# The order of ScalarE's and VectorE's work on a bank of transposed rows

## The chip, the cores and the metric

The kernel runs on one core of one Trainium2 chip. The metric is the device time of one execution in microseconds (us). A core has five engines with an instruction queue each, worked off in order: TensorE (PE in the profile; its weight loads are PEld), VectorE (DVE), ScalarE (ACT), GpSimd (POOL) and SyncE (SP). Matmul results land in PSUM, which has eight banks; a bank holds 512 f32 numbers in each of 128 partitions.

## The reference, cut to what matters

One layer of a decoder is computed for a prompt of 1024 rows and for eight sample rows with a paged cache of 8192 positions each. The change touches the prompt alone, at the two places where normed rows go into the next projection:

```
xp = xp + merge_heads(fox_prompt(...), sgu_prompt(...), g_att_out, g_sgu_out, w_o)
xp = xp + cross_attend(rmsnorm(xp, g_cross), mk, mv, w_cq, w_co)
f, conv_p = conv_ffn(rmsnorm(xp, g_ffn), zeros, w_up, conv_w, conv_b, w_down)
xp = xp + f
```

The model width is 1024 and all numbers are f32.

## The kernel before, in words

**Products.** Each large product is made of three matmuls in a reduced format: every f32 operand is split into a rounded part h and a remainder l, and h·h + h·l + l·h is summed (`gemm3`, lines 272 to 274). The helper `split` makes the two parts. ScalarE rounds (line 235, or line 238 where each row is multiplied by a gain on the way), and VectorE subtracts the rounded part from the source (line 236, or 239 with the gain). Weights come through SyncE's queue into buffers `wr` (line 249) and are split into `wh` and `wl` on lines 235 and 236.

**Tiling of the prompt.** The 1024 rows are worked on in two halves of 512 rows. For each half there is an output projection (`out_proj`, lines 1063 to 1065 and 1081 to 1083), then cross attention (`cross`), a second output projection inside it, and the MLP (`ffn`). A half has four blocks of 128 rows.

**The seam.** `norm_T` turns the finished rows so that the next product can use them. It is called four times in the kernel: into cross attention and into the MLP, for each half of the prompt. One call goes through two pairs of row blocks (`t0` = 0 and 2), and in each pair through four banks (`kk` = 0, 2, 4, 6). Into one bank TensorE puts four transposes of 128x128 (line 1124): columns 0 to 255 belong to feature block kk, columns 256 to 511 to feature block kk+1. `split` is then called once for each half of the bank (line 1129), with the gain of that feature block. So one call of `norm_T` has 8 banks and 16 splits, and the kernel has 64.

In the text below A0 and A1 are ScalarE's roundings of the first and second half of a bank (line 238, 128x256), and V0 and V1 are VectorE's remainders of these halves (line 239, 128x256).

**What comes behind a seam.** After the four banks of a pair, `first` runs the first product of the next stage on these 256 columns (`gemm3_late`): first all matmuls that need only rounded rows (lines 280 and 281), then those that need the remainders (line 284). The products after it go through `gemm3`.

**What comes ahead of it.** The second output-projection column goes block by block; the sum with the residual is line 1015, its squares are line 230, and `factor` (line 1031 on ScalarE, line 1032 on GpSimd) gives the scale of a row block, which `scaled` (line 1037) or, for the last two blocks, `both` (line 1044 on ScalarE, line 1045 on VectorE) applies. The last pair of transposes waits for `both`; eight matmuls without use (`fill`, line 1102) stand ahead of them.

**What sets the order.** The program is written as generators that yield an estimated duration; a loop at the end mixes in the steps of the sample rows (the decode), whose VectorE work on gathered cache pages is on lines 1444 and 1448, whose matmuls into `dv` are on line 1495, and whose gathers GpSimd issues on lines 1428 and 1489. The framework then orders the instructions of every engine by a simulated timeline when the kernel is built, with priorities (`tc.high_priority` stands around the transposes and the splits of a bank), and adds the waits between engines. On the chip this order is fixed.

Of the kernel before, what the change touches and what calls it, by code (L numbers as in the profile page):

```python
# [7 lines left out]
F32 = mybir.dt.float32  # L8
# [3 lines left out]
AF = mybir.ActivationFunctionType  # L12
ALU = mybir.AluOpType
# [65 lines left out]
def build(nc, tc, ctx, a, phases=None):  # L79
# [31 lines left out]
    def U(shape, dt=F32):  # L111
        n = 1
        for s in shape[1:]:
            n *= s
        t = upool.tile([P, UW], dt, tag="u", bufs=NU, name=nm("u"))[:, :n]
        if len(shape) == 3:
            t = t.rearrange("p (a b) -> p a b", b=shape[2])
        return t
# [50 lines left out]
    gp = const.tile([P, G_W], F32, tag="gp", name="gp")  # L169
# [62 lines left out]
    def split(src, h, l, scale=None):  # L232

        if scale is None:
            nc.scalar.activation(h, src, AF.Copy)  # L235
            nc.vector.tensor_tensor(l, src, h.bitcast(F32), op=ALU.subtract)  # L236
        else:
            nc.scalar.activation(h, src, AF.Copy, scale=scale)
            nc.vector.scalar_tensor_tensor(l, src, scale, h.bitcast(F32), op0=ALU.mult, op1=ALU.subtract)  # L239
# [858 lines left out]
    def fill(tr, hs):  # L1098

        for k in range(8):  # L1100
            with tc.issue_after(newest(ENG.PE)):
                mmul(tr[:, :256], hs[k][:, 0:P], hs[k][:, 0:256], start=True, stop=True)

    def norm_T(ys, g0, first):


        hs, ls = [], []
        for t0 in (0, 2):
            c = slice(t0 * P, (t0 + 2) * P)
            late = callable(ys[t0])  # L1110
            if late:
                ys[t0:] = ys[t0]()
            for kk in range(0, 8, 2):
                if t0 == 0:
                    h2, l2 = U([P, 2, 512], F32R), U([P, 2, 512], F32R)
                    hs += [h2[:, 0, :], h2[:, 1, :]]
                    ls += [l2[:, 0, :], l2[:, 1, :]]
                tr = TR()
                if late and kk == 0:
                    fill(tr, hs)  # L1120
                with tc.high_priority():
                    for q in range(2):
                        for i in range(2):
                            nc.tensor.transpose(
                                tr[:, (q * 2 + i) * P : (q * 2 + i + 1) * P], ys[t0 + i][:, (kk + q) * P : (kk + q + 1) * P], ident
                            )
                    for q in range(2):
                        k = kk + q
                        split(tr[:, q * 256 : (q + 1) * 256], hs[k][:, c], ls[k][:, c], scale=gp[:, g0 + k : g0 + k + 1])
                yield 0.6  # L1130
            first(hs, ls, c)
            if t0 == 0:
                yield 3
        held[0] = False
        return hs, ls


    def cross(xt, sq):
# [19 lines left out]
        def first(hs, ls, c):  # L1158
            gemm3_late([(ps[:, c], pairs(ws, d, hs, ls, c)) for d, ps in enumerate(begun)])

        hs, ls = yield from norm_T(xt, G_CROSS, first)
        r = rows_rstd(sq, 0, 4)
        rq = sm([P, 4], "rq", 2)
# [105 lines left out]
    def ffn(hf, xt, ys, late=None):  # L1269
# [6 lines left out]
        def first(hs, ls, c):  # L1276
            gemm3_late([(pv[:, c], pairs(w, hs, ls, c)) for w, pv in begun.values()])

        hs, ls = yield from norm_T(ys, G_FFN, first)
        if hf:  # L1280

# [753 lines left out]
```

## Time and profile before

| | |
|---|---|
| time, median of 3 runs | 1794.42 us (1788.66 to 1794.93) |
| time of the profiled execution | 1793.69 us |
| its span in the profile | 1791.7 us, so 2.0 us lie around it |
| TensorE clock over the span | 0.993 of full speed |
| VectorE, ScalarE, GpSimd busy | 78%, 41%, 27% of the span |
| cross attention, first and second half | seams at about 521 to 548 us and 1154 to 1187 us |
| MLP, first and second half | seams at about 684 to 708 us and 1321 to 1343 us |

A row of the timeline gives the start in us, the duration, the engine, the line of the kernel, the operation, output and inputs with their shapes, the number of instructions merged in the row, and in brackets how long the engine stood idle ahead of it and what ended that. Instructions on ScalarE and VectorE overlap a little at their ends, so the next one of the same kind starts 0.1 us before the one ahead of it has ended.

### The profile page before, as it was taken

How to read it: one execution, taken by the hardware profiler on the slowest of the kernel's cores; microseconds unless marked ns; L12 is line 12 of the kernel's file. 1: busy time of each engine (PE TensorE's matmuls, PEld its weight loads, DVE VectorE, ACT ScalarE, POOL GpSimd, SP SyncE). 2: the span in 40 equal slices, each digit the busy share in tenths (PEclk: the TensorE clock that was granted, in tenths of full speed). 3: DMA queues.
4: the chain of work that ended last, by engine and by line, in shares of the span. 5: the costliest groups of instructions: out<-in, count | busy, mean ns of one | idle time of the engine just before them, and what ended most of it. 6: DMA issues, size and time to landing. Idle time of an engine off the chain costs nothing.

```text
span 1791.7 us, 25124 instructions
## 1 busy us (share of the span) xinstructions
PE 1735.9 (97%) x9653; PEld 1285.7 (72%) x9653; DVE 1399.9 (78%) x1733; ACT 733.5 (41%) x1374; POOL 488.3 (27%) x461
## 2 busy tenths in 40 slices
PE   8999999889999999999999999999999999999997
PEld 5787777655677666767777777766666778768875
DVE  4689658989788986989999999898885549855344
ACT  6332355566643635333333244335353233333232
POOL 1252234443222332333322223433322112102110
PEclk9999999999999999999999999999999999999999
DMA  8786798777697975779788788988879587568982
GB/s 291 297 304 226 294 334 319 259 264 244 254 403 279 363 299 224 282 285 345 290 301 313 291 317 311 376 306 346 320 280 350 214 306 249 191 260 297 359 310 80
DMA packets 157074, 521.06 MB, mean 291 GB/s; under 512 B 20874, under 2 KB 40842, under 8 KB 124186
## 3 DMA queue, kind: packets, MB, share of 16 engines
q0 software_dynamic: 57168, 341.14, 50.0%
q1 hardware_dynamic: 92874, 165.73, 26.5%
q10 hardware_dynamic: 6912, 12.59, 1.9%
q8 instruction: 76, 1.25, 0.3%
q14 instruction: 44, 0.36, 0.1%
HBM read 495.47 MB, written 23.93 MB: 290 GB/s over the span
## 4 chain that ended last, share of the span: by engine, by line
PE 53%; issue 9%; DMA 8%; DVE 6%; ACT 2%; POOL 2%; POOLq 0%; DVEq 0%; ACTq 0%; SPq 0%
DMA kv<-cache_v,io 6%; PE ba L272 6%; PE ba L274 6%; PE ba L273 6%; PE dv L1495 4%; PE bb L272 3%; PE bb L273 3%; PE bb L274 3%; PE ba L1063 1%; DVE s L1448 1%; PE ba L1064 1%; PE ba L1065 1%; PE dv L331 1%; DMA kv<-cache_k,io 1%; PE dv L1774 1%
## 5 line engine op out<-in xcount | busy, mean ns | idle before, releaser
L235 ACT ACTIVATE wh<-wr 128x1024 fp32r<-128x1024 f32 (+2 forms) x220 | 228.6, 1044 | 443.3 <-PE ba L273 142.3
L236 DVE TENSOR_TENSOR wl<-wr,wh 128x1024 fp32r<-128x1024 f32 (+2 forms) x220 | 262.7, 1200 | 165.1 <-PE ba L274 57.4
L1428 POOL DMA_INDIRECT kv<-cache_k,io x128 | 186.9, 1460 | 606.8 <-DVE s L1448 327.2
L1444 DVE TENSOR_TENSOR kv<-kv,d 128x1024 f32<-128x1024 f32 (+1 forms) x156 | 258.0, 1681 | 32.6 <-DMA kv<-cache_k,io 32.6
L1448 DVE TENSOR_REDUCE s<-kv 128x16 f32<-128x1024 f32 (+1 forms) x156 | 258.4, 1672 | 0.0
L1489 POOL DMA_INDIRECT kv<-cache_v,io x128 | 160.8, 1256 | 239.4 <-PE dv L1495 155.2
L272 PE MATMUL ba<-u,wh 128*128 128x512 f32 x528 | 209.3, 397 | 0.0
L274 PE MATMUL ba<-u,wl 128*128 128x512 f32 x528 | 209.0, 396 | 0.0
L273 PE MATMUL ba<-u,wh 128*128 128x512 f32 x528 | 208.5, 395 | 0.5 <-DVE u L239 0.5
L272 PE MATMUL ba<-wh,u 128*128 128x512 f32 (+1 forms) x495 | 186.1, 379 | 0.9 <-ACT u L235 0.9
L273 PE MATMUL ba<-wl,u 128*128 128x512 f32 (+1 forms) x495 | 185.1, 375 | 1.3 <-DVE wl L236 1.3
L274 PE MATMUL ba<-wh,u 128*128 128x512 f32 (+1 forms) x495 | 183.4, 375 | 0.0
L1495 PE MATMUL dv<-kv,s 128*32 128x512 f32 x1024 | 127.1, 598 | 1.6 <-DMA kv<-cache_v,io 1.6
L274 PEld LDWEIGHTS ba<-u,wl 128*128 128x128 f32 x528 | 99.2, 188 | 29.0 <-issue 6.5
L272 PEld LDWEIGHTS ba<-u,wh 128*128 128x128 f32 x528 | 99.3, 188 | 26.4 <-issue 4.8
L273 PEld LDWEIGHTS ba<-u,wh 128*128 128x128 f32 x528 | 99.2, 188 | 25.2 <-issue 2.3
L272 PEld LDWEIGHTS ba<-wh,u 128*128 128x128 f32 x495 | 93.0, 188 | 25.0 <-issue 6.5
L272 PE MATMUL bb<-u,wh 128*128 128x512 f32 x272 | 108.7, 400 | 0.0
L274 PE MATMUL bb<-u,wl 128*128 128x512 f32 x272 | 108.0, 398 | 0.0
L273 PE MATMUL bb<-u,wh 128*128 128x512 f32 x272 | 107.9, 397 | 0.0
L273 PEld LDWEIGHTS ba<-wl,u 128*128 128x128 f32 x495 | 93.0, 188 | 20.1 <-DVE wl L236 1.9
L274 PEld LDWEIGHTS ba<-wh,u 128*128 128x128 f32 x495 | 92.9, 188 | 19.5 <-issue 1.6
(454 smaller groups left out, 3310.6 us busy)
## 6 DMA issues: line engine op xcount, KB each, us to landing
wr<-w_up SPq DMA_DIRECT2D x88, 512.0 KB
kv<-w_up POOLq DMA_DIRECT2D x22, 1024.0 KB
wr<-w_down SPq DMA_DIRECT2D x40, 512.0 KB
kv<-w_down POOLq DMA_DIRECT2D x11, 1024.0 KB
wr<-w_in SPq DMA_DIRECT2D x16, 512.0 KB
wr<-w_o SPq DMA_DIRECT2D x16, 512.0 KB
wr<-w_cq SPq DMA_DIRECT2D x16, 512.0 KB
wr<-w_co SPq DMA_DIRECT2D x16, 512.0 KB
```

The costliest lines, as they stand in the source:

```text
L235: nc.scalar.activation(h, src, AF.Copy)
L236: nc.vector.tensor_tensor(l, src, h.bitcast(F32), op=ALU.subtract)
L272: mmul(out, sh, mh, start=(i == 0), stop=False)
L273: mmul(out, sh, ml, start=False, stop=False)
L274: mmul(out, sl, mh, start=False, stop=(i == n - 1))
L331: mmul(ps[32 * j : 32 * j + 32, :w], xT[:, k, :] if nk == 8 else xT[:, k * 8 : k * 8 + 32], raw[:, q, j * w : (j + 1) * w], start=(k == 0) ...
L1063: mmul(pss[i], mh[k][:, tb], wh, start=(k == korder[0]), stop=False)
L1428: nc.gpsimd.indirect_dma_start(kv, None, a["cache_k"], off(kidx[:, b, ch : ch + 1]))
L1444: nc.vector.tensor_tensor(kvv[:, i : i + m, :], kvv[:, i : i + m, :], qb.unsqueeze(1).broadcast_to((P, m, 512)), op=ALU.mult)
L1448: nc.vector.tensor_reduce(s[:, ch * 4 + i : ch * 4 + i + m, :].rearrange("p k h -> p (k h)"), kvv[:, i : i + m, :].rearrange("p k (h d) -> ...
L1489: nc.gpsimd.indirect_dma_start(kv, None, a["cache_v"], off(kidx[:, b, ch : ch + 1]))
L1495: mmul(dv[32 * j : 32 * j + 32, :], s[:, ch * 4 : ch * 4 + 4, :].rearrange("p k h -> p (k h)"), kvv[:, j, :], start=(ch == 1), stop=(ch == ...
```

## The change

In `norm_T` the two calls of `split` on a bank are written out and put in another order: both of ScalarE's roundings first, then both of VectorE's remainders. The operations, their operands and their number stay.

```diff
-                    for q in range(2):
-                        k = kk + q
-                        split(tr[:, q * 256 : (q + 1) * 256], hs[k][:, c], ls[k][:, c], scale=gp[:, g0 + k : g0 + k + 1])
+                    gain = [gp[:, g0 + k : g0 + k + 1] for k in (kk, kk + 1)]
+                    src = [tr[:, q * 256 : (q + 1) * 256] for q in range(2)]
+                    for q in range(2):
+                        nc.scalar.activation(hs[kk + q][:, c], src[q], AF.Copy, scale=gain[q])
+                    for q in range(2):
+                        nc.vector.scalar_tensor_tensor(
+                            ls[kk + q][:, c], src[q], gain[q], hs[kk + q][:, c].bitcast(F32), op0=ALU.mult, op1=ALU.subtract
+                        )
```

The roundings stand on line 1130 of the changed kernel and the remainders on line 1132; what stood on lines 235, 238 and 239 for other callers stays there, and all lines behind move down by five.

## The prediction

> **What bounds the kernel now.** The first part of the page gives the busy time of each engine.
>
> ```profile
> span 1791.7 us, 25124 instructions
> ...
> PE 1735.9 (97%) x9653; PEld 1285.7 (72%) x9653; DVE 1399.9 (78%) x1733; ACT 733.5 (41%) x1374; POOL 488.3 (27%) x461
> ```
>
> TensorE is idle for 1791.7 − 1735.9 = 55.8 us, 3% of the span. The change takes no work from TensorE, so it can only give back idle TensorE time, or time in which TensorE ran below full clock. How much of this lies at the seams? The view of waits, for TensorE alone, was read over the four seams. Over the first one (512 to 549 us) it has no row; the others follow in order of time (engine, its line, whom it waited for: sum, times, longest).
>
> ```profile
> PE bb L1124 <- ACT u L1044: 1.7, 1, 1.7
> PE ba L280 <- ACT u L238: 1.2, 3, 0.6
> PE ba L280 <- DVE u L239: 0.6, 1, 0.6
> ```
> ```profile
> PE bb L280 <- ACT u L238: 1.7, 1, 1.7
> PE ba L273 <- DVE u L239: 0.5, 1, 0.5
> ```
> ```profile
> PE ba L280 <- DVE u L239: 1.1, 1, 1.1
> PE ba L1124 <- ACT u L1044: 0.8, 1, 0.8
> PE ms L1616 <- DVE s L1483: 0.5, 1, 0.5
> PE bb L1124 <- DVE u L1045: 0.2, 1, 0.2
> PE ba L284 <- DVE u L239: 0.2, 1, 0.2
> ```
>
> Roundings and remainders stand for 1.8 us at the second seam, 2.2 at the third and 1.3 at the fourth, 5.3 us together; the scale of the last rows (L1044, L1045) for 2.7 more. The view of windows puts this beside the granted clock (columns: window, its length, busy time of PE, PEld, DVE, ACT, POOL with counts, PE clock, DMA share, GB/s).
>
> ```profile
> 532.00:541.00 9.00, 9.00 (x47) 7.52 (x46) 9.00 (x13) 4.36 (x8) 0.94 (x1) 1.00 0.99 381
> 692.00:697.00 5.00, 3.12 (x21) 2.39 (x19) 3.97 (x8) 3.37 (x8) 0.57 (x1) 1.00 1.02 425
> 697.00:700.00 3.00, 1.65 (x10) 1.46 (x11) 1.02 (x3) 2.97 (x10) 0.55 (x1) 0.93 1.01 422
> 700.00:704.00 4.00, 4.00 (x25) 4.00 (x24) 2.10 (x6) 0.63 (x4) 1.01 (x1) 0.63 0.60 245
> 1176.00:1181.00 5.00, 2.95 (x17) 2.38 (x18) 5.00 (x9) 2.14 (x6) 0.94 (x1) 1.00 1.01 398
> 1322.00:1326.00 4.00, 3.38 (x24) 1.23 (x22) 3.96 (x7) 1.97 (x6) 2.67 (x3) 1.00 0.94 364
> 1326.00:1331.00 5.00, 3.62 (x26) 3.21 (x27) 4.75 (x11) 4.29 (x10) 0.56 (x1) 1.00 1.01 412
> 1331.00:1335.00 4.00, 3.26 (x28) 2.77 (x27) 2.72 (x6) 2.70 (x9) 0.55 (x1) 1.00 0.96 398
> 1335.00:1343.00 8.00, 8.00 (x51) 6.40 (x55) 4.19 (x9) 2.89 (x8) 0.00 (x0) 1.00 0.02 7
> ```
>
> At the first seam TensorE is full (9.00 of 9) with out-projection matmuls; a faster seam is worth nothing there. The idle time elsewhere is 1.88 + 1.35 us at the second seam, 2.05 at the third, 0.62 + 1.38 + 0.74 at the fourth: 8.0 us. From 700 to 704 us the clock was 0.63, so 4 × 0.37 = 1.5 us of work was lost though TensorE counts as busy. All that the change could touch is therefore 8.0 + 1.5 = 9.5 us.
>
> **What the present order costs.** At the third seam ScalarE and TensorE show:
>
> ```profile
> 1172.34 0.47 ACT L238 ACTIVATE u<-bb,gp 128x256 fp32r<-128x256 f32 x1 [0.20 <-PE bb L1124]
> ...
> 1178.99 0.47 ACT L238 ACTIVATE u<-bb,gp 128x256 fp32r<-128x256 f32 x1 [2.19 <-DVE u L239]
> ```
> ```profile
> 1176.21 2.35 DVE L1444 TENSOR_TENSOR kv<-kv,d 128x1024 f32<-128x1024 f32 x2
> 1178.49 0.47 DVE L239 SCALAR_TENSOR_TENSOR u<-bb,gp,u 128x256 fp32r<-128x256 f32 x1
> ```
> ```profile
> 1179.52 0.39 PE L280 MATMUL bb<-u,wh 128*128 128x256 f32 x1 [1.70 <-ACT u L238]
> ```
>
> A0 of the `bb` bank ran at 1172.34, A1 of the same bank only at 1178.99, though the transposes of both halves had long ended. A1 waited for V0, and V0 stood in VectorE's queue behind two decode instructions of 2.35 us together. A1 reads other columns and writes another half of the output than V0 reads, so no value passes from V0 to A1: what they share is the bank, which the planner hands from one engine to the other in program order. Line 280 needs only rounded rows, yet it pays for VectorE's queue.
>
> **The change part by part.** Nothing is added or taken away: 64 roundings and 64 remainders of 0.47 us each, no DMA issued, none moved past another in SP's or GpSimd's queue. Per bank the handings between the engines fall from three (A0, V0, A1, V1) to one (A0, A1, V0, V1). ScalarE no longer waits for VectorE; V0 now waits for A1. The four seams:
>
> *First seam:* 0, covered by the out-projection matmuls of the window above. Without that cover it would be worth up to the two ScalarE waits of this kind there, which I leave to the rivals.
>
> *Second seam:*
>
> ```profile
> 694.98 0.47 ACT L238 ACTIVATE u<-bb,gp 128x256 fp32r<-128x256 f32 x1 [0.43 <-PE bb L1124]
> 695.35 0.29 ACT L1031 ACTIVATE fac<-sqx,part 128x1 f32<-128x1 f32 x1
> 696.32 1.33 ACT L1044 ACTIVATE u<-u,fac 128x512 f32<-128x512 f32 x2 [0.68 <-POOL fac L1032]
> ...
> 698.17 0.45 ACT L238 ACTIVATE u<-bb,gp 128x256 fp32r<-128x256 f32 x1
> ```
> ```profile
> 697.71 0.33 PE L1124 MATMUL bb<-cp,u 128*128 128x128 f32 x1 [1.70 <-ACT u L1044]
> 698.68 0.39 PE L280 MATMUL ba<-u,wh 128*128 128x256 f32 x1 [0.64 <-ACT u L238]
> 698.90 0.28 PE L281 MATMUL ba<-u,wl 128*128 128x256 f32 x1
> 699.02 1.46 PE L284 MATMUL ba<-u,wh 128*128 128x256 f32 x8
> ```
>
> Here the last A1 was ordered behind the scale of the next rows and ran 3.2 us after its A0. In the new order it follows at 695.35. The ten matmuls that need it (698.68 to 700.48, 1.8 us) then fill the 1.70 us in which TensorE waited for L1044, and the 0.64 us go too: −2.3. In turn L1031 and all behind it (GpSimd's power, L1044, the first transpose) come one rounding later, 695.35 − 694.98 = 0.37: +0.4. With the idle time closed the clock should not drop: −1.5. Sum −3.4. Ends: +0.4, if the chain of L1044 sets the time whatever fills the gap, and −4.7, if the whole idle 3.2 us of the two windows and the clock's 1.5 come back.
>
> [...]
>
> *Third seam:* A1 follows A0, L280 finds its rows: −1.7. The 0.5 us of L273 waiting for a remainder stay. Ends: 0, if V1 is the next thing late (V0 and V1 still stand behind the same decode work, and line 284 and all `gemm3` need them), and −2.05, the window's idle time.
>
> *Fourth seam:*
>
> ```profile
> 1322.01 0.47 ACT L238 ACTIVATE u<-ba,gp 128x256 fp32r<-128x256 f32 x1 [1.10 <-PE ba L1124]
> 1322.38 0.47 ACT L238 ACTIVATE u<-bb,gp 128x256 fp32r<-128x256 f32 x1
> 1322.73 0.48 ACT L238 ACTIVATE u<-ba,gp 128x256 fp32r<-128x256 f32 x1
> 1325.23 0.84 ACT L238 ACTIVATE u<-ba,gp 128x256 fp32r<-128x256 f32 x2 [2.02 <-DVE u L239]
> ```
>
> Three A0 run back to back, then ScalarE stands for 2.02 us until VectorE has done its first V0. Behind it in ScalarE's queue are the other roundings, a weight rounding, squares and the scale of the last rows. All come up to 2.0 us earlier: −1.1 for L280, and −1.0 of the 0.8 + 0.2 for L1044 and L1045. Sum −2.1; ends 0 and −2.74 (the idle time of the three windows). The earlier weight rounding frees its load buffer earlier; its transfer meets a DMA share of 1.01 and gains nothing, and after the seam (share 0.02) none is missing.
>
> *New wait:* V0 behind A1, 0.37 us. Queued behind V0 are V1 and decode work; who waits is line 284 or L273. It is hidden where line 280 and 281 run first. I charge it twice, where remainders are waited for today (L273, L284): +0.7. Ends: 0, and 0.37 × 8 row-block pairs = +3.0.
>
> Sum: −3.4 − 1.7 − 2.1 + 0.7 = −6.5. The ends add up to +3.4 and −9.5. On the profiled execution's own time of 1793.69 (span 1791.7 and 2.0 around it) this gives 1787.2; that execution stood 0.7 below the median of 1794.42. I take **1787**, 0.4% below the median.
>
> **The rivals.**
>
> *More than the sum.* The planner sees roundings come free early and moves all that follows on ScalarE. In its favour: of ScalarE's idle time
>
> ```profile
>   DVE u L239: 11.7, 7
> ```
>
> ended with a remainder, in 7 waits, and only 2.19 + 2.02 of it is used above. If half of the other 7.5 us reached TensorE, the sum is −6.5 − 3.8 = −10.3, so 1783. Against it: the first seam's window shows TensorE full.
>
> *VectorE is next late.* In the window of the third seam VectorE is busy 5.00 of 5, at the fourth 3.96 of 4. If every remainder sets the pace, the gains shrink to the second seam's 2.3 us less the 0.7 for V0: 1792, no change.
>
> *Slower: the planner is too hopeful.* The order of all engines is made anew from simulated times. Seeing rounded rows early, it may put lines 280 and 281 into TensorE's queue ahead of out-projection matmuls that cover the seam today; on the chip A1 still stands behind a weight rounding, and TensorE, in order, waits. The place is the first pair of each seam; the price per misplacement is between the 1.7 us of the third seam and TensorE's largest wait for a remainder (far from the seams, at 250 us):
>
> ```profile
> PE ba L306 <- DVE u L239: 7.1, 1, 7.1
> ```
>
> The mechanism decides from four such waits of their mean of 4.4 us on: 4 × 4.4 = 17.6, less the sum's 6.5 is +11, so 1805. Four waits of 1.7 would only cancel the gain. For it: such an order is fixed when the kernel is built and cannot adapt. Against it: the program order and the priorities are the same.
>
> *The change does nothing.* If the planner kept A1 behind V0 for another reason than the bank, the time is 1794.
>
> **How the numbers follow.** Anything within 0.5% of the median (1785.4 to 1803.4) can't be told from no change here. The forecast gets 0.46 (0.22 faster by over 0.5%, since it lies 1.6 us above that edge and its lower end reaches 1784; 0.24 within); more than the sum 0.22, all faster; VectorE late 0.04 and nothing done 0.02, both within; slower 0.26. That is 0.44, 0.30 and 0.26. The range runs from 1776, where both the lower end of 9.5 us and the whole 7.5 us are given back (1793.7 − 17.0), to 1809, five misplacements less the sum (5 × 4.4 − 6.5 = 15.5 over 1793.7); the likeliest case's own range is 1784 to 1797.
>
> **What would show it.** In the changed kernel ScalarE's roundings on line 1130 should no longer show idle time that ends with a remainder; A1 should follow A0 by about 0.37 us; the 1.70 us wait of L280 at the third seam, the 2.02 us ScalarE wait at the fourth and the 3.2 us between A0 and A1 at the second should be gone; the clock around the second seam should stay at 1.00. The prediction is wrong if TensorE's idle time at the seams is as large as now with remainders named in place of roundings, if a seam's window shows a new TensorE wait of over 2 us, or if the time moves in stretches far from the seams.

## The result, and the profile after

| | before | after |
|---|---|---|
| median of 9 runs each | 1794.08 us (1788.66 to 1795.85) | 1803.98 us (1795.74 to 1807.39) |
| ratio | | 1.0051, 95% interval 1.0032 to 1.0070 |
| profiled execution, its span | 1793.69 us, 1791.7 us | 1795.74 us, 1794.0 us |

The change made the kernel about 0.5% slower where 0.4% faster was forecast. The profiled execution of after is the fastest of its nine, so its trace shows only part of the loss. The first part of its page reads:

```profile
span 1794.0 us, 25148 instructions
...
PE 1734.5 (97%) x9653; PEld 1284.6 (72%) x9653; DVE 1398.5 (78%) x1733; ACT 731.2 (41%) x1374; POOL 506.4 (28%) x461
```

Four engines have the work they had. GpSimd, which the change does not touch, is busy 18 us longer with the same 461 instructions (506.4 against 488.3), and 17 of these 18 us lie in its gathers of cached keys and values. This is no chance of one execution: over all traces of this text GpSimd is busy 479 to 494 us in the five with the old order at every seam, and 497 to 512 us in the nine with the new order at some seam. That line is the first hint at the cause; the seams come first here, since the forecast spoke of them.

**At the banks the change does what it says.** ScalarE in the timeline of after (the changed kernel), around the second, third and fourth seam:

```profile
694.44 0.84 ACT L1130 ACTIVATE u<-bb,gp 128x256 fp32r<-128x256 f32 x2 [0.81 <-PE bb L1124]
```
```profile
1171.03 0.84 ACT L1130 ACTIVATE u<-bb,gp 128x256 fp32r<-128x256 f32 x2 [0.30 <-PE bb L1124]
```
```profile
1321.02 1.58 ACT L1130 ACTIVATE u<-ba,gp 128x256 fp32r<-128x256 f32 x4
```

A0 and A1 stand in one row each time, and no rounding waits for a remainder any more: the 3.2 us between them at the second seam, TensorE's 1.70 us at the third and ScalarE's 2.02 us at the fourth are gone.

**The gain at the MLP seams does not get past the next gate.** The view of windows of after (columns as in the prediction), over the same stretches or those of them that moved by a few microseconds:

```profile
692.00:697.00 5.00, 4.34 (x32) 3.75 (x30) 4.34 (x7) 2.90 (x7) 0.57 (x1) 1.00 1.01 426
697.00:700.00 3.00, 1.49 (x11) 1.26 (x11) 0.17 (x1) 2.94 (x8) 0.55 (x1) 1.00 1.02 429
700.00:704.00 4.00, 3.62 (x17) 3.54 (x18) 2.87 (x9) 2.80 (x9) 1.01 (x1) 0.57 0.54 219
1172.00:1177.00 5.00, 4.13 (x31) 3.38 (x29) 5.00 (x6) 2.50 (x6) 0.00 (x0) 1.00 0.90 319
1322.00:1326.00 4.00, 3.97 (x30) 2.86 (x23) 4.00 (x8) 1.67 (x3) 3.39 (x3) 1.00 0.98 377
1326.00:1331.00 5.00, 3.36 (x24) 2.66 (x23) 4.33 (x11) 2.52 (x6) 1.19 (x2) 1.00 0.97 361
1331.00:1335.00 4.00, 2.52 (x13) 2.19 (x14) 2.60 (x5) 2.02 (x7) 0.54 (x1) 0.61 0.97 403
1335.00:1343.00 8.00, 8.00 (x46) 7.16 (x48) 4.12 (x9) 2.37 (x7) 0.00 (x0) 0.77 0.06 27
```

TensorE's idle time here sums to 6.6 us where it was 8.0, but the clock takes 1.7 + 1.6 + 1.8 us (4 × 0.43, 4 × 0.39, 8 × 0.23) where it took 1.5: 11.7 us in all against 9.5. TensorE's waits at the second and the fourth seam, and the chain that ends the fourth one's longest, on VectorE and on ScalarE; last, where this chain began before:

```profile
PE ba L1124 <- DVE u L1045: 1.2, 1, 1.2
PE ba L1124 <- ACT u L1044: 0.8, 1, 0.8
PE ba L280 <- ACT u L1130: 0.6, 1, 0.6
```
```profile
PE bb L1124 <- DVE u L1045: 1.2, 1, 1.2
PE bb L1124 <- ACT u L1044: 1.0, 1, 1.0
PE ba L284 <- DVE u L1132: 0.6, 1, 0.6
```
```profile
1326.86 0.67 DVE L1015 TENSOR_TENSOR u<-ba,u 128x512 f32<-128x512 f32 x1
...
1332.43 0.88 DVE L1045 TENSOR_SCALAR u<-u,fac 128x512 f32<-128x512 f32 x2 [0.46 <-POOL fac L1032]
```
```profile
1327.56 0.63 ACT L230 ACTIVATE junk<-u 128x512 bf16<-128x512 f32 x1 [2.10 <-DVE u L1015]
...
1329.51 1.33 ACT L1044 ACTIVATE u<-u,fac 128x512 f32<-128x512 f32 x2 [0.89 <-POOL fac L1032]
1330.74 0.61 ACT L230 ACTIVATE junk<-u 128x512 bf16<-128x512 f32 x1
...
1331.48 0.29 ACT L1031 ACTIVATE fac<-sqx,part 128x1 f32<-128x1 f32 x1
```
```profile
1326.68 0.68 DVE L1015 TENSOR_TENSOR u<-ba,u 128x512 f32<-128x512 f32 x1
```

Counted from the last matmul of the output projection ahead of the seam, the first pair of row blocks now ends 3.7 us earlier at the second seam and 1.4 at the fourth (4.4 and 0.5 when the second executions of both kernels, below, are compared). The second pair needs the scale of both last row blocks, and this is one chain: the residual sum of the third block (line 1015), its squares (line 230), its scale on ScalarE (line 1044), and only behind this the squares and the factor of the fourth block, whose scale on VectorE (line 1045) ends the wait. At the fourth seam the chain did not start earlier: its line 1015 began 2.9 us behind the last matmul of the output projection (which ended at 1324.00), before 1.4 us behind it (1325.27). What TensorE won it stands idle for, and in this execution the clock then fell to one half for 3.4 and 6.8 us. In a second execution of after the gate was the same and these two falls did not come.

### The profile page after: what moved, and what is told of

It is laid out like the page before. It is cut to its first block, busy times and chain, and to the rows that moved or that the text cites. A ratio compares the mean times of both kernels' runs of the same rounds, so it can differ in the third digit from the quotient of the medians.

```text
span 1794.0 us, 25148 instructions
## 1 busy us (share of the span) xinstructions
PE 1734.5 (97%) x9653; PEld 1284.6 (72%) x9653; DVE 1398.5 (78%) x1733; ACT 731.2 (41%) x1374; POOL 506.4 (28%) x461
## 4 chain that ended last, share of the span: by engine, by line
PE 59%; DVE 8%; issue 6%; DMA 5%; ACT 2%; POOL 1%; DVEq 0%; POOLq 0%; ACTq 0%; SPq 0%
PE ba L272 8%; PE ba L274 8%; PE ba L273 8%; PE dv L1500 4%; PE bb L272 4%; PE bb L274 4%; PE bb L273 4%; DMA kv<-cache_k,io 1%; DVE kv L1449 1%; PE ba L1064 1%; PE ba L1063 1%; PE ba L1065 1%; PE dv L331 1%; PE dv L1779 1%; DMA kv<-cache_v,io 1%
## 5 line engine op out<-in xcount | busy, mean ns | idle before, releaser
L235 ACT ACTIVATE wh<-wr 128x1024 fp32r<-128x1024 f32 (+2 forms) x220 | 228.7, 1044 | 482.5 <-PE ba L273 144.6
L1433 POOL DMA_INDIRECT kv<-cache_k,io x128 | 195.3, 1526 | 569.3 <-DVE s L1453 318.3
L1494 POOL DMA_INDIRECT kv<-cache_v,io x128 | 169.7, 1326 | 262.9 <-PE dv L1500 156.3
```

The lines of the kernel that those rows point to most:

```text
L1433: nc.gpsimd.indirect_dma_start(kv, None, a["cache_k"], off(kidx[:, b, ch : ch + 1]))
L1494: nc.gpsimd.indirect_dma_start(kv, None, a["cache_v"], off(kidx[:, b, ch : ch + 1]))
```

## The experiments

Three readings stood against each other at first: A, the gate and the clock at the MLP seams; B, the re-planned work in cross attention; C, chance of single executions. The first four kernels separate the seams.

**1 and 2: both kernels again.** No edit.

> The kernel before, unchanged, timed against itself, for its clock and its spread. Three theories of why the changed kernel came out slower (median 1803.98 against 1794.08 us). A, gate and clock: at the MLP seams the first pair's product ends earlier, but the second pair still waits for the scale of the last two row blocks, so the gain turns into idle TensorE time ahead of it, and the granted clock falls to one half there more often. B, re-planned cross attention: the new order of the engines costs time in the scores of cross attention. C, chance: half-clock stretches fall at random in the attention stage, which both kernels share instruction for instruction, and the difference is drawn from them. Expected here by all three: ratio 1.000 within 0.2%. C expects single executions up to 1805 us and clocks down to 0.989 as the changed kernel had; A and B expect none over 1798 and clocks of 0.992 to 0.996.

> The changed kernel, unchanged, again. A and B: ratio to before of 1.004 to 1.007, as in the first measurement. C: ratio of 1.000 to 1.002. A also expects half-clock stretches inside 1328 to 1340 us of the profile in this execution too, B none of importance there.

Before: 1793.09 us (12 runs), ratio 1.0012 (0.9991 to 1.0034) to the other runs of before in the set, whose median was 1791.13. After: 1801.95 us (8 runs), 1.0057 (1.0035 to 1.0079). The loss is real, so C falls as its explanation; single runs of before did reach 1803. The stretches at half clock that A expected at 1328 to 1340 us in the second trace of after did not come.

**3 and 4: the new order at one kind of seam alone.**

```
both_first = g0 == G_FFN      # 3; G_CROSS in 4
for q in range(2):
    nc.scalar.activation(hs[kk + q][:, c], src[q], AF.Copy, scale=gain[q])
    if not both_first: nc.vector.scalar_tensor_tensor(...)
for q in range(2 if both_first else 0): nc.vector.scalar_tensor_tensor(...)
```

> The new order at the two MLP seams alone, the old one at the two seams into cross attention. A: the whole loss is here, ratio 1.004 to 1.006. B: ratio 0.999 to 1.001. C: 1.000. In the profile A expects the first pair's last remainder product (L284) of the fourth seam to end 2 us earlier than before in its stage, the last transposes to start within 0.5 us of before, and at least one half-clock stretch of 3.4 us behind them.

> The new order at the two seams into cross attention alone. A: no loss or a small gain, ratio 0.998 to 1.001, since the second pair there has no scale to wait for. B: the loss is here, ratio 1.003 to 1.006, with the scores of the first half (about 577 to 622 us before, 44.6 us long) 3 to 4 us longer. C: 1.000.

MLP seams alone: 1796.40 us, 1.0029 (1.0013 to 1.0045). Cross-attention seams alone: 1796.99 us, 1.0036 (1.0021 to 1.0051). Neither A nor B alone: each had expected the whole loss in one of the two kernels, and both lose. Their sum, 0.65%, is near the 0.57% of the whole change, but the table below shows that the losses do not add stage by stage. To see where, each trace was cut at fixed matmuls, for instance the first cross stage (the first cross attention) from the end of the last matmul of line 1081 ahead of its seam to the end of its last product with the values (line 1216 of before). Its two ends in before, and then in after:

```profile
539.88 0.40 PE L1081 MATMUL ba<-wh,u 128*128 128x512 f32 x1
...
639.65 1.02 PE L1216 MATMUL bb<-u,t 128*128 128x512 f32 x2
```
```profile
536.22 0.39 PE L1081 MATMUL ba<-wh,u 128*128 128x512 f32 x1
...
639.70 1.02 PE L1221 MATMUL bb<-u,t 128*128 128x512 f32 x2
```

100.4 us before, 104.1 after. All stages so cut, as the difference to the trace of before (us); two in which no trace differs by over 0.1 us are left out:

| trace | up to seam 1 | first cross stage | MLP 1 with seam 2 | to seam 3 | second cross stage | MLP 2 with seam 4 |
|---|---|---|---|---|---|---|
| before again | −3.6 | −0.1 | +0.5 | −0.8 | +0.9 | −2.0 |
| after | −3.7 | **+3.7** | +1.4 | −2.4 | 0.0 | +3.2 |
| after again | −3.0 | **+4.7** | −1.0 | −2.0 | +5.6 | −0.2 |
| MLP seams alone | −4.0 | **+4.7** | −1.0 | −1.4 | +4.3 | −0.2 |
| cross seams alone | −3.2 | **+3.5** | +0.3 | −0.5 | −2.7 | +4.2 |

Ahead of the first seam the planned order is the same in all of them: before's profiled execution was simply 3 to 4 us slow there, which hid most of the loss in the first comparison. The steady loss is 3.5 to 4.7 us in the first cross stage. It stands even in the one trace of the kernel with the MLP seams alone, whose order is the same as before's on every engine until 682 us. So in that trace it cannot be the order of the banks; something else comes late, and the old order can meet it too.

**What comes late there: a gather that occupies GpSimd for longer.** VectorE and GpSimd of after, then the same stretch of before:

```profile
602.31 1.21 DVE L1449 TENSOR_TENSOR kv<-kv,d 128x1024 f32<-128x1024 f32 x1
603.44 2.35 DVE L236 TENSOR_TENSOR wl<-wr,wh 128x1024 fp32r<-128x1024 f32 x2
605.71 1.21 DVE L1453 TENSOR_REDUCE s<-kv 128x16 f32<-128x1024 f32 x1
...
613.77 1.22 DVE L1449 TENSOR_TENSOR kv<-kv,d 128x1024 f32<-128x1024 f32 x1 [2.85 <-DMA kv<-cache_k,io]
```
```profile
602.65 3.94 POOL L1433 DMA_INDIRECT kv<-cache_k,io  x1 [4.05 <-DVE s L1453]
```
```profile
603.32 1.67 POOL L1428 DMA_INDIRECT kv<-cache_k,io  x1 [0.54 <-DVE s L1448]
```
```profile
602.97 2.35 DVE L1444 TENSOR_TENSOR kv<-kv,d 128x1024 f32<-128x1024 f32 x2
...
612.63 1.22 DVE L1444 TENSOR_TENSOR kv<-kv,d 128x1024 f32<-128x1024 f32 x1
```

The gather of cached keys occupied GpSimd for 3.94 us instead of 1.67. (It also began later, 66.0 us into the stage instead of 63.0.) It ended at 606.59, 0.88 us after VectorE had begun the reduction of 605.71; until then VectorE ran a decode product and two weight remainders without a pause. VectorE then stood 2.85 us for the gathered keys. Behind this wait in its queue is the maximum of the cross-attention scores; ScalarE waits for it (line 1198) and has behind it the copy of the next keys of cross attention (line 1180), for which TensorE waits (line 1193):

```profile
616.76 0.48 ACT L1198 ACTIVATE cbs<-cmx,rq 128x1 f32<-128x1 f32 x2 [1.31 <-DVE cmx L1195]
...
618.17 0.59 ACT L1180 ACTIVATE t<-ba 128x512 f32<-128x512 f32 x1
```
```profile
604.80 1.65 PE L1193 MATMUL bb<-t,u 128*128 128x256 f32 x3 [2.01 <-ACT t L1180]
...
618.81 3.50 PE L1193 MATMUL ba<-t,u 128*128 128x256 f32 x15 [1.82 <-ACT t L1180]
```

The wait at 604.80 has the same source one gather earlier. In after, then in before:

```profile
567.36 5.09 POOL L1433 DMA_INDIRECT kv<-cache_k,io  x1 [0.60 <-DVE s L1453]
```
```profile
580.62 2.36 DVE L1449 TENSOR_TENSOR kv<-kv,d 128x1024 f32<-128x1024 f32 x2 [4.34 <-DMA kv<-cache_k,io]
```
```profile
574.12 0.94 POOL L1428 DMA_INDIRECT kv<-cache_k,io  x1 [5.01 <-DVE s L1448]
```
```profile
582.35 2.36 DVE L1444 TENSOR_TENSOR kv<-kv,d 128x1024 f32<-128x1024 f32 x2 [1.80 <-DMA kv<-cache_k,io]
```

Counted from the last matmul of line 1081 (ending 536.6 in after, 540.3 in before), VectorE got its keys at 44.0 us instead of 42.1, and the copy ahead of TensorE's wait came at 67.6 instead of 65.7. The kernel with the MLP seams alone, with before's planned order, had the same at another gather:

```profile
599.92 5.08 POOL L1438 DMA_INDIRECT kv<-cache_k,io  x1 [1.67 <-DVE s L1458]
```

Is that the order or chance? Ten traces have the old or the new order in this stage (the six above and the four of experiments 5 to 8). In all five with the new order there, the gather at 567 us took 5.09 us and that at 602 us 3.94 or 3.95, and the stage was 3.5 to 6.0 us longer than in before. With the old order the first took 0.94 us in all five and the second 1.67 or 1.68 in four, and the stage was within 0.7 us of before's; the fifth is the kernel with the MLP seams alone, with the 5.08 us just shown. In that trace and in the second one of before the gather began 0.35 us behind the start of the same decode product, and it passed in the second one of before alone. So the new order held both gathers each time, and the old one held the second once in five.

The same ten traces show that VectorE's instruction at the start of a gather decides (counted where that instruction had begun at least 0.05 us before and went on for at least 0.4 us more; of the first two rows' kind, 6 more gathers began within 0.03 us of the instruction and passed in 0.94 us):

| VectorE at the gather's start | gathers | ended within 1.05 us | median us |
|---|---|---|---|
| decode product (line 1444), both operands in the core's memory | 392 | 0 | 2.40 |
| weight remainder (line 236), the same | 302 | 0 | 1.68 |
| decode reduction (line 1448), one operand | 262 | all | 0.94 |
| instruction with an operand in a bank | 107 | all | 0.94 |

A held gather ended 0.8 to 0.9 us behind the end of an instruction of VectorE in 66 of 68 cases of the first two rows in the trace of before and in 73 of 77 in that of after, nearly the 0.94 us that a gather of the last two rows takes in all. Where two such instructions followed each other at once and the gather began during the first (at any time), the change let it through in 203 of 318 cases; in the others it waited on. The rows show that the gather is held (0 of 694 passed); by what, and which part of its work, no run shows.

**5 and 6: decode products and reductions in turn.** Theory L, the held gather, against G, the gate and the clock at the MLP seams.

```
 for i in range(0, 4, m):
     nc.vector.tensor_tensor(kvv[:, i : i + m, :], ..., op=ALU.mult)
-for i in range(0, 4, m):
     nc.vector.tensor_reduce(s[:, ch * 4 + i : ...], ..., op=ALU.add)
```

> The new order, and in the decode scores each half's reduction (L1448 of before) now stands right behind its product (L1444 of before) instead of both products ahead of both reductions, so that VectorE no longer runs two of them in a row. Theory L, 'the gather is held': in the four traces with an edit so far, GpSimd's gather of cached keys at about 600 us took 3.9 to 5.1 us instead of 1.67, ending 0.9 us after the first instruction of VectorE that is neither L1444 nor the weights' L236; VectorE then waits 2.4 to 3.4 us for it at 613, and TensorE 3.8 to 4.7 us for ScalarE's keys copy in the stage, with a stretch at half clock in three of the four. L expects: the wait of VectorE for the gather in the first cross stage under 1.5 us, TensorE's waits for the keys copy there under 2 us, and the time 3 to 6 us under the new order's 1802, that is 1796 to 1799. Theory G, 'gate and clock at the MLP seams': the loss sits where the second pair waits for its scale, and this kernel stays at 1800 to 1804.

> The same interleaving of decode products and reductions in the kernel before. L: gathers come earlier there too, but the two traces of before had little of this wait in the first cross stage (1.2 to 1.6 us of TensorE), so 0 to 3 us faster, 1788 to 1791, and the difference to the new order with the same interleaving is 3 to 8 us where it was 10. G: no change, 1790 to 1793, the difference stays at 10.

With the new order 1798.72 us (6 runs), 1.0052 (1.0033 to 1.0071); in the old order 1791.77 (12 runs), 1.0005 (0.9992 to 1.0017). The difference is 7.0 us, where it was 8.9 in experiments 1 and 2. The edit missed its target: in both traces every engine works off the same operations on the same tiles, in the same order, as without it. A product and two remainders still stood where the gather came (3.95 us again at 603.2). So the two runs are third executions of after and of before, and that 1798.72 lies in L's range and not in G's decides nothing. As repeats they show how much one order can vary: the second cross stage of this old order was 6.9 us longer than before's, with a gather of 6.22 us in it.

**7 and 8: TensorE kept busy ahead of the second pair at the MLP seams.** In `fill`, `range(24)` in place of `range(8)`, with `hs[k % 8]`; the products are not used.

> The new order, with 24 matmuls in place of 8 whose results are not used, put ahead of the second pair's transposes at each MLP seam (0.12 us each, so 1.9 us more; the two waits that they would fill are 0.77 and 1.21 us in the trace of the new order). G expects: the waits ahead of the second pair go, the stretch at half clock behind them too, the second pair ends within 0.3 us of where it did without the stretch, and the time falls by 1 to 4 us to 1798 to 1801. L, and a third view that the clock's stretches there are worth nothing on average: no change or up to 1 us slower, 1801 to 1804.

> The same 24 matmuls in the kernel before, where TensorE waits only 0.2 to 0.7 us ahead of the second pair: both theories expect 1.9 us at each MLP seam less what of it falls into waits, so 1 to 4 us slower, 1792 to 1795; by G with the stretch at half clock behind seam 2 gone in exchange, up to 2 us back.

New order: 1796.86 us (7 runs), 1.0032 (1.0017 to 1.0047), against 1.0057 without (1.0035 to 1.0079, so the intervals overlap). Old order: 1797.87 (11 runs), 1.0038 (1.0024 to 1.0052), 6 us slower. The first is faster than G had expected, the second slower than both theories had. In the trace with the new order the 1.21 us wait is gone at the second seam, and there is no half clock behind it; at the fourth a wait of 1.54 us and the half clock behind it stayed. This trace does not bear G out: at the second seam the half clock was also missing in the second and third execution of after, where the wait was there. The first cross stage kept both held gathers and was 6.0 us longer than before's, so the time gained lies elsewhere. And the old order lost more than the added matmuls cost (2 × 1.9 us), and its trace has 5 gathers of over 3.5 us behind the first seam where those of before have 2 and 1: each re-made plan brings its own.

**9 and 10: the runs on VectorE broken.**

```
def gap(tag):
    prev = next(i for i in reversed(nc.cur_bb.bb.instructions) if i.engine == ENG.DVE)
    with tc.high_priority(), tc.issue_after(prev):
        nc.vector.tensor_reduce(sm([P, 1], tag, ...), ident[:, 0:2], axis=AX.X, op=ALU.max)
```

called behind each split of a `w_co` weight and, while a half of the prompt is between attention and its MLP, behind each decode product.

> The interleaved run left the pair of instructions in question where it was: at 602 to 605 us the new order still ran L1444 L236 L236 in a row and the gather took 3.95 us, so it told nothing of theory L. Here the run itself is broken: behind each product of the decode scores and behind each remainder of w_co in the stages from the first seam on, VectorE makes a reduction of two elements of a constant into a scratch of one element (104 in all, results unused). In ten traces a gather that began while VectorE ran L1444 or the weights' L236 (two operands in the core's memory) never ended within 1 us, and nearly always 0.8 to 0.9 us after that run; one that began during a reduction or an instruction with an operand in a bank took 0.94. L expects: in the first cross stage the gather at about 602 under 2.8 us in place of 3.95, VectorE's wait for it under 1.7 us in place of 2.4 to 3.4, TensorE's waits for the keys copy under 3 us in place of 3.8 to 5.3 in the five traces with the new order there, and 1797 to 1800 where the new order has 1802. Rival N, 'the wait has another source' (ScalarE's own queue ahead of the keys copy): the gather may be shorter, TensorE's waits stay at 3.8 to 5.3 and the time stays at 1801 to 1805.

> The same small reductions in the kernel before, which had 1.2 to 1.7 us of these waits in the first cross stage in four traces: L expects 1790 to 1794 (no more than 2 us off 1791.5 either way), so that the difference between the two orders falls from 10 us to 4 to 8. N: the difference stays at 10.

New order: **1794.02 us** (12 runs), 1.0006 (0.9992 to 1.0019). Old order: 1790.55 (12 runs), 0.9996 (0.9986 to 1.0006); the difference between the orders is 3.5 us, where L had expected 4 to 8 and N 10. The new order gains 8 us on its 1801.95, more than L had expected, and the loss is no longer measurable. TensorE's waits in the first cross stage of the new order, and GpSimd and VectorE at the place in question:

```profile
PE dv L1509 <- DMA kv<-cache_v,io: 0.9, 1, 0.9
...
PE ba L1200 <- ACT t L1187: 0.2, 1, 0.2
```
```profile
601.72 0.94 POOL L1440 DMA_INDIRECT kv<-cache_k,io  x1 [1.71 <-DVE s L1462]
```
```profile
601.37 0.68 DVE L1202 TENSOR_REDUCE cmx<-ba 128x2 f32<-128x512 f32 x1
601.96 2.35 DVE L1456 TENSOR_TENSOR kv<-kv,d 128x1024 f32<-128x1024 f32 x2
604.23 0.15 DVE L244 TENSOR_REDUCE gapk<-cp 128x1 f32<-128x2 f32 x1
```

The waits for the keys copy fell from 3.8 us to 0.2, the stage is 0.9 us longer than before's instead of 3.7, and the rival N (another source of the wait) falls. At this spot, though, the gather was not let through by a break: the re-made plan had the maximum of the scores (an operand in a bank) there.

**11: the new order with the breaks and 24 matmuls in `fill`.**

> The new order with both: the small reductions on VectorE and 24 matmuls instead of 8 ahead of the second pair at the MLP seams, which alone took the new order from 1802 to 1796.9. If the two losses are separate (the gather in the cross stages, the gate and the clock at the MLP seams) the gains add: 1791 to 1795, no slower than before. If both only shake the plan, anything from 1795 to 1802.

1791.79 us (12 runs), 0.9995 (0.9985 to 1.0005): level with before, and faster than neither kernel by more than the interval. Against experiment 9 it is 0.1% less, with intervals that overlap.

**12: breaks that themselves use two operands.** As in 9, with `tensor_tensor(..., ident[:, 0:1], ident[:, 1:2], op=ALU.max)`.

> The new order with the same 104 small instructions as in the run of 1794.0, but each takes the maximum of two operands in the core's memory in place of reducing two elements: VectorE's order stays the same but for a few places, and the runs of two-operand instructions are no longer broken. In the trace of that run the gather at 601.7 began while VectorE ran L1190 of before (operand in a bank) instead of L1444, and took 0.94 us; the small reduction itself let the gather of 588.9 through at 1.67 us and did not help that of 570.7 (3.01 us). Theory 'break' (the small reductions give GpSimd its moment): gathers in the cross stages over 2.5 us come back, and the time goes to 1798 to 1803. Theory 'order' (what counts is which instruction of VectorE a gather meets, and the small instructions only moved it): the gather at 602 stays at 0.9 to 1.7 us, TensorE's waits for the keys copy in the first cross stage under 1 us, time 1792 to 1797.

1798.18 us (12 runs), 1.0024 (1.0008 to 1.0040). The number is in the range of "break", the trace does not bear its reason out. Where one of the added small instructions stood directly between two of the long ones, the gather went through in all 10 cases here, as in all 35 of the traces of 9 to 11; so it is not the operands of the short one alone that decide. (Where another small instruction followed it, at 569 to 571 us in three traces, the gather did not go through and took 3.0 us.) Small instructions that the kernel had anyway do not all let a gather through: a sum of 128x8 with two operands in the core's memory (0.15 us) never did, in 6 of 6 cases over all traces. Here is one in the trace of experiment 9:

```profile
1070.39 3.66 POOL L1440 DMA_INDIRECT kv<-cache_k,io  x1 [6.46 <-PE dv L1509]
```
```profile
1069.76 2.27 DVE L1456 TENSOR_TENSOR kv<-kv,d 128x2048 f32<-128x2048 f32 x1
1071.95 0.15 DVE L1425 TENSOR_TENSOR tot<-d,lfz 128x8 f32<-128x8 f32 x1
1072.03 1.20 DVE L236 TENSOR_TENSOR wl<-wr,wh 128x1024 fp32r<-128x1024 f32 x1
```

Moreover, a few places of the plan had moved: at 601.65 the gather met two decode products with nothing between them and took 2.81 us. "Order" expected 0.9 to 1.7 there, so it fell as well in its details; what both share, that it depends on what VectorE works on when a gather comes, stands.

Set side by side, with the number of gathers of over 3.5 us behind the first seam in the one trace of each kernel (the medians come from four sets of runs, in which before's own was 1791.1 to 1793.2, and the first one of after from a fifth, with 1794.1):

| kernel | gathers over 3.5 us | first cross stage, us more than before | median us |
|---|---|---|---|
| before again; decode in turn (same order); broken runs | 1; 2; 2 | −0.1; 0.7; 0.9 | 1793.1; 1791.8; 1790.6 |
| before with 24 in `fill` | 5 | 0.1 | 1797.9 |
| MLP seams alone; cross seams alone | 6; 4 | 4.7; 3.5 | 1796.4; 1797.0 |
| after; again; decode in turn (same order) | 6; 9; 9 | 3.7; 4.7; 6.0 | 1804.0; 1802.0; 1798.7 |
| after with 24 in `fill` | 3 | 6.0 | 1796.9 |
| after, broken runs; with 24 in `fill`; two operands | 4; 1; 3 | 0.9; 1.3; 2.2 | 1794.0; 1791.8; 1798.2 |

**The clock's part.** The lost time can be split by the mean granted clock of all executions: the time times (1 − clock) is, as an estimate, the most that TensorE can have lost to half clock (the 128x128 transposes of after began 0.11 us apart at 698.7 us, at full clock, and 0.21 apart at 701.7, at half). Before: 8.5 us of 1792.0 (mean of 29 runs); after again: 13.3 of 1801.3 (8 runs); with broken runs: 7.8 of 1794.1 (12 runs). So of the 9.3 us, up to 4.8 are clock, and at least 4.5 are idle time. With the breaks the clock's part is gone, and 2.3 us of the other remain (1794.1 − 7.8 = 1786.3, against 1784.0 for before in that set). In the trace of after the half-clock stretches begin at 604.8 and 700.4 us, where waits of 2.0 and 1.2 us had just ended, and at 1331.9, between two waits of 1.0 and 1.2.

Over all 14 traces the half clock moved rather than only grew. Around the second seam (692 to 704 us) a stretch lies in all six traces with the old order at the MLP seams, and in one of the eight with the new order, that of after shown above. Around the fourth seam (1323 to 1343 us) it is one of six and five of eight. In the first cross stage a stretch lies in five of the six traces in which that stage was 3.5 us longer or more, and in none of the eight others.

## Why the prediction was wrong, step by step

- *A0 and A1 one behind the other, the waits for remainders gone:* right at each seam, to the row. *The clock at 1.00 around the second seam (−1.5):* wrong in the profiled execution (0.57), right in the other seven traces with the new order there, while all six with the old order have the half clock. So this term came true; its size is rather 1.7, half of one stretch of 3.4 us, since the window of 697 to 700 us with its 0.93 holds the rest. That closing the idle time keeps the clock up was an estimate, and no run shows it: the second and third execution of after had the wait at this seam and not the half clock. And half clock came up at the fourth seam and in cross attention, which the sum had at nothing.
- *First seam 0:* right.
- *Second seam −3.4:* the first pair moved 3.7 us, but the second pair gave back 4.2 (2.9 in the second execution). The failed step is that the ten matmuls "then fill the 1.70 us in which TensorE waited for L1044": they ran earlier, at 694.97 to 696.8, and two waits for the scale (0.77 and 1.21 us) opened behind them. The seam is then worth little: in the second execution, without half clock, the second pair ends 0.8 us earlier than in before, counted from the last matmul of the output projection.
- *Fourth seam −2.1:* the failed step is "All come up to 2.0 us earlier". Of the term of −1.0 for L1044 and L1045 nothing came; their waits grew from 0.8 + 0.2 to 1.0 + 1.2 us. The scale's chain begins with line 1015 on VectorE and came no earlier (2.9 us into the seam instead of 1.4): the second pair's transposes start at 1332.97 instead of 1333.42, in a stage that had itself begun 1.3 us earlier.
- *Third seam −1.7:* 1.1 us of TensorE's idle time did go, 2.2 to 1.1; by the end of that cross stage it had gone elsewhere (0.0 in the table).
- *New wait of V0 behind A1, +0.7:* not seen. The waits of lines 284 and 273 for a remainder at the seams fell from 0.7 us (0.2 and 0.5) to 0.6 (line 284 at the fourth seam), and there V0 and V1 stood behind decode work (line 1467), not behind A1.
- *The rival "planner too hopeful"* had the right sign and the right source, an order made anew from simulated times, but the wrong place and price. No misplaced line 280 or 281 waited: none of their waits at the seams was over 0.6 us. What went wrong is the fetching of decode data in cross attention, far from the banks, and its price is 3.5 to 6.0 us in the first cross stage. The price that the prediction took was unsound too: the 7.1 us wait of L306 ends at 7.15 us, at the start of the kernel, not at 250 us as written there.

*The step that failed most* is none of the four seams: the sum has everything outside them at nothing, on the ground that "no DMA issued, none moved past another". GpSimd's order did stay the same until 1126 us, but VectorE's did not, and with it two gathers of the first cross stage were held, and the stage took 3.5 to 6.0 us more, in all five traces with the new order there.

The prediction's own last sentence named what happened: the time moved "in stretches far from the seams". What it missed was in the page of before. The gathers' groups there, and in after:

```profile
L1428 POOL DMA_INDIRECT kv<-cache_k,io x128 | 186.9, 1460 | 606.8 <-DVE s L1448 327.2
```
```profile
L1433 POOL DMA_INDIRECT kv<-cache_k,io x128 | 195.3, 1526 | 569.3 <-DVE s L1453 318.3
```

The mean of 1460 ns against a shortest of 0.93 us says that gathers are often held, so a new order can hold others; the forecast looked at the order of the queues, not at what holds a gather in its place.

What stays open: how much of the loss is the MLP seams' own. With the breaks in, 24 matmuls in `fill` brought 0.1%, without them 0.25%, both with intervals that overlap, and the second with half clock still there at one seam of two. Nor was it tried why a gather passes between two long instructions in 203 cases of 318. The traces give one sign: where the second one's record began 0.069 to 0.072 us before the end of the first, none of 45 passed, otherwise 203 of 273. Nor is it known what made before's own plan fall well. The breaks are no clean test either: they changed the plan, and in experiment 9 the gather at 602 us was spared by the new plan and not by a break.

## What to carry to other kernels

Before you count what a wait is worth, look for the gate behind it: here the scale of the last rows, on another engine and in another queue, took back at once what the first pair had won. In a kernel ordered by a planner, an edit can change the order of the whole rest (or, as in experiments 5 and 6, of nothing); compare the orders first, then the stages with a second run of each kernel, and find out what in the old order was luck. Where GpSimd issues gathers, count long two-operand instructions in a row on VectorE as part of the gather's time (here 3.94 us where a decode product and two weight remainders ran, in place of 1.67).

## What the runs showed of the hardware

- A gather on GpSimd never ended within 1.05 us when it had begun at least 0.05 us into a decode product or a weight remainder on VectorE (1.2 us or more, both operands in the core's memory): 0 of 694 in ten traces, with medians of 2.40 and 1.68 us. During a reduction of the decode (line 1448), or an instruction with an operand in a bank, its median was 0.94 us and it always ended within 1.05 us (369 of 369).
- One added VectorE instruction of 0.15 us between two such long ones let the gather through in 45 of 45 cases, also when it had two operands there; a sum of 128x8 of the same length did so in none of 6.
- The granted clock was either full or half (1.0 or 0.5) in all 14 traces, in stretches of 3.4 or 6.8 us inside the kernel, and in each trace the stretches began whole multiples of 3.413 us apart (11, 15 and 112 of them behind the first in before, 28 and 213 in after). Waits of 1.0 to 2.0 us went with such a stretch in the first execution of after, and the wait at its second seam came without one in the next. The spread of single runs, 1786.5 to 1803.8 us for before, can be the clock's in part: with a mean granted clock of 0.997 and 0.992 in these two, at most 9 of the 17 us by the estimate above.
